# Tile 2's threshold by taking away eight smallest scores sixteen times, and a priority for each kind of step in attention's list

## The chip, the cores and the metric

The kernel runs on one core of a Trainium2 chip. A core has a matrix engine (TensorE, in the profile PE, with its weight loads as PEld), a vector engine (VectorE, DVE), an activation engine (ScalarE, ACT), a general engine (GpSimd, POOL) and a queue that issues transfers (SyncE, SP). They run side by side and wait for each other by semaphores. The metric is the device time of one execution, in microseconds.

## The reference

One decoder layer for 1024 tokens of width 1024. A conditioning vector gives shifts, scales and gates. One input projection gives q, k, v for 8 heads of 64, the queries, keys and weights of a small indexer, and 512 pooling channels. The indexer scores every earlier token for every query, and attention sees only the best 256:

```python
score = jnp.einsum('bqh,bqhs->bqs', w, jax.nn.relu(logits))
score = jnp.where(causal[None], score, -jnp.inf)
_, idx = lax.top_k(score, k_sel)          # k_sel = 256
...
s = jnp.where(valid[:, None], s, -jnp.inf)
p = jax.nn.softmax(s, axis=-1)
o = jnp.einsum('bhqk,bqkhd->bhqd', p, vg.astype(jnp.float32))
```

Attention and pooling go through an output projection, a gated residual and a layer norm; then a SwiGLU with inner width 2816, a second gated residual and a second layer norm.

## The kernel before, in words

The 1024 queries are 8 tiles of 128 (numbered 0 to 7). Tile i has 128 (i + 1) keys in causal reach. Tiles 0 and 1 have at most 256 and need no selection. For tiles 2 to 7 the kernel makes the indexer's scores (`score(i)`, fp32, one row for each query), finds the 256th largest score of each row as a threshold, and then overwrites the scores with a mask: 0 where the key is taken, a large negative number where not. Attention adds the mask to its own scores.

**The threshold** is found bit by bit in `bisect` (line 569). A first pass counts the scores that are not negative, which gives the sign. Then a search over 15 bits of the upper half of the fp32 word and one over 16 bits of the lower half: for each bit a pass over the row compares keys (16-bit integers in `keys[i]`) with a candidate and counts, and two small instructions set the next candidate. In `search_v` (line 600) all of this runs on DVE, in `search_a` (line 614) the pass and the small steps run on ACT. Tiles 3 and the pair 5, 4 are searched on ACT, tile 2 and the pair 7, 6 on DVE. The end of `bisect` (lines 648 to 666) makes the mask: equal and less-than flags, a scan that settles ties from the right, and the final product.

`bisect` is a generator: each `yield` names an engine and an estimate of the next piece. Before attention, `fill` (line 702) puts pieces into gaps of the projections. Tile 2's search is the late one (`LATE`, line 49): it takes pieces only when tiles 7 and 6 are done.

**Attention** has 32 units, from the largest tiles down: (7, 6) for four head pairs, then (5, 4), (3, 2), (1, 0). A unit, in `unit` (line 1199), has these steps, each a task of a list:

- `s`: scores of two heads on PE, into one or two of the two wide banks.
- `x`: scores plus mask, with the row maximum, on DVE (in the profile CUSTOM_DVE_ANT_0, sm from s and score). Frees the bank.
- `e`: exponential with row sum, on ACT.
- `r`: reciprocal on DVE. `n`: the product with it on POOL.
- `p`: transposes of the probabilities on PE, up to four to a bank (pT). `c`: the copy out of that bank, on ACT or DVE.

For each head pair follow `o` (the product with v on PE), `hi` (rounded copy on ACT) and `lo` (the remainder on DVE). `q_rows` (line 1162) prepares the queries of tiles 5 to 0: `load` from memory, `turn` (transposes on PE), and copies `own` and `other` on ACT and `low` on DVE, written to qab. Banks for `turn`, `p` and `o` come from a ring of four.

**The order** is written out by a planner that runs while the kernel is built (lines 1300 to 1378). It keeps a clock for each engine, knows what every task needs, and picks, again and again, the task that can start earliest; among equal starts the lowest rank goes first, where the rank of unit k's tasks is about 10 k. A piece of a search that is not finished is a candidate too (`Chain`, line 1284), with a rank that rises toward the unit that needs the mask. A task with two engines pays `V_BIAS` on the second: 0.15, on DVE. The order that comes out is fixed on PE, DVE, ACT and POOL; the engines keep it whatever the real durations are. An `x` task waits in the planner for its tile's mask, and `turn` for the masks whose buffers its output overwrites.

Behind the list come the output projection (`wo`), layer norm, and the SwiGLU, whose matmuls (`gu`, `dn`) fill TensorE to the end.

Every instruction goes through one helper, so the profile gives line 178 for nearly all; they are told apart by the names of their tiles.

Of the kernel before, what the change touches and what calls it, by code (L numbers as in the profile page):

```python
# [20 lines left out]
P = 128  # L21
# [19 lines left out]
EAGER = 0  # L41
Q_LEAD = 40
CHAIN_LEAD = 1
V_BIAS = 0.15
AHEAD_SMALL = 2
NORM = 2
NORM_SMALL = 2
# [87 lines left out]
class Queue:  # L135
# [6 lines left out]
    def cost(self, op, aps, k):  # L142
        out, n = aps[0], 1
        for s_ in out.shape[1:]:
            n *= s_
        if self.name == "T":
            if op == "transpose":
                return 0.13
            return max(n * (0.000443 if aps[1].dtype == F32R else 0.0000131 * aps[1].shape[-1]), 0.11)
        if self.name == "A":  # L150
            return max(0.26, 0.14 + n * 0.00088) + (0.31 if "accum_out" in k else 0)
        if self.name == "G":
            return 0.12 + n * {"tensor_tensor": 0.00225, "scalar_tensor_tensor": 0.0014}.get(op, 0.00125)
        if out.dtype in (BF16, I16, U16) and op in ("tensor_scalar", "tensor_tensor", "tensor_copy"):
# [36 lines left out]
def decoder_layer_kernel(  # L191
# [23 lines left out]
    def buf(where, off, n, name, dt=F32):  # L215
        return nc.alloc_sbuf_tensor_at(f"{name}_{where}{off}", [P, n], dt, offset=area[where] + 4 * off).ap()
# [327 lines left out]
    def score(i):  # L544
        return XS[:, s_off[i] : s_off[i] + P * (i + 1)]
# [21 lines left out]
    biased, hold = set(), []  # L567

    def bisect(tiles, cols, on_act):

        nt = len(tiles)
        col = lambda q: cols[:, q * 4 : q * 4 + nt]
# [4 lines left out]
        def trash(i):  # L577
            return ((junkA if 5 in tiles else junkB) if on_act else junkd(i))[:, 0 : P * (i + 1)]
# [67 lines left out]
        V.tensor_tensor(th.bitcast(I32), th.bitcast(I32), ib.bitcast(I32), ALU.bitwise_or)  # L646
        V.tensor_tensor(M, th, sg, ALU.mult)
        for m, i in enumerate(tiles):
            n = P * (i + 1)
            sc = score(i)  # L650
            T1 = one(M, m)
            eq, lt = kv[i].bitcast(BF16), trash(i)
            yield "V", 1.7 * w_(i) + 0.1

            V.tensor_scalar(eq, sc, T1, None, ALU.is_equal)
            V.tensor_scalar(lt, sc, T1, float(TOPK - n), ALU.is_lt, ALU.add, accum_out=one(ng, m))
            V.tensor_scalar(one(ng, m), one(ng, m), -0.5, None, ALU.add)
            yield "V", 1.6 * w_(i)
            left = sc.bitcast(BF16)[:, 0:n]
            V.tensor_tensor_scan(left[:, ::-1], eq[:, ::-1], eq[:, ::-1], one(ng, m), ALU.add, ALU.bypass)  # L660
            V.tensor_scalar(left, left, 0.0, None, ALU.is_lt)
            yield "V", 1.8 * w_(i)
            V.tensor_tensor(eq, eq, left, ALU.mult)
            V.tensor_tensor(lt, lt, eq, ALU.max)
            V.tensor_scalar(sc, lt, NOT_TAKEN, None, ALU.mult)
            biased.add(i)


    queues = {"V": V, "A": A, "G": G}
# [450 lines left out]

    class Task:

        def __init__(self, q, cost, rank, emit, deps=(), slots="", late=0.0):
            self.q, self.cost, self.rank, self.emit, self.deps, self.slots, self.late = q, cost, rank, emit, deps, slots, late
            self.end, self.kind, self.masks = None, emit.__name__[0:2], ()

    class Ring:

# [33 lines left out]
    def q_rows(t, rank):  # L1162
        hold_ = {}

        def load():
            hold_["raw"] = q_load(t)

        def turn():
            hold_["pt"] = q_transpose(hold_["raw"])

        b = qab[t]
        qa, ql = b[:, 0:1024], b[:, 1024:1536]
        qops[t] = qa, ql
# [15 lines left out]
        l_ = task("S", 0.1, rank, load, q_turns[-3:-2], late=4.0)  # L1189
        t_ = task("T", 0.55, rank, turn, (l_,), "A", late=0.2)  # L1190
        c0 = task("A", 1.2, rank, lambda: copies(0), (t_,))
        lw = task("V", 1.4, rank, lambda: copies(2), (c0,))
        c1 = task("A", 1.2, rank, lambda: copies(1), (c0,))
        t_.readers = (c1, lw)
        t_.masks = {1: (2, 3), 0: (4, 5)}.get(t, ())
        q_done[t] = (c1, lw)
        q_turns.append(t_)

    def unit(k):
# [23 lines left out]
        xs = [task("V", 0.08 + 0.00105 * n, 10 * k, lambda e=e: x_(e), [s_t] + before, late=0.12) for e in (0, 1)]  # L1223
        for x in xs:
            x.masks = (i,)
        s_t.readers = xs
        es = [task("A", 0.16 + 0.00097 * n, 10 * k + 1, lambda e=e: e_(e), (xs[e],), late=0.15) for e in (0, 1)]
        r_ = task("V", 0.15, 10 * k + 1, lambda: V.reciprocal(cols["c"][:, 2:4], cols["c"][:, 2:4]), es, late=0.15)
        ns = [task("G", 0.1 + 0.001 * n, 10 * k + 2, lambda e=e: n_(e), (r_,), late=0.15) for e in (0, 1)]
        ps, cs = [], []  # L1230
        for e in (0, 1):
            for j0 in range(0, i + 1, 4):
# [13 lines left out]
                    else:  # L1246
                        A.activation(dst, pv, AF.Copy)

                p = task("T", 0.107 * m, 10 * k + 3, p_, (ns[e],), "A", late=0.25)
                c = task("AV", (0.09 + 0.11 * m, 0.09 + 0.13 * m), 10 * k + 3, c_, [p] + list(o_tasks[-2:-1]), late=0.1)  # L1250
                p.readers = (c,)
                ps.append(p)
                cs.append(c)
# [8 lines left out]
    for k in range(0, nu, 2):  # L1262
# [15 lines left out]
        h_t = task("A", 0.3, 10 * k + 15, hi_, (o_t,), late=0.1)  # L1278
        l_t = task("V", 0.38, 10 * k + 16, lo_, (h_t,), late=0.1)
        o_t.readers = (l_t,)  # L1280
        o_tasks.append(o_t)
    goal = {2: 17, 3: 16, 4: 9, 5: 8, 6: 1, 7: 0}

    class Chain:

        def __init__(self, st):
            self.st, self.at, self.n = st, 0.0, -1
            nt = len(st[3])
            total = 6 * nt + 1 + (31 * (nt + 1) + 2 if st[5] else 31 * nt)
            self.left = max(total - st[6], 1)  # L1290
            self.goal = max(goal[i] for i in st[3]) - CHAIN_LEAD
# [13 lines left out]
    for i in biased:  # L1305
        masked[i] = 0.0
    chains = [Chain(st) for st in streams]
    todo.sort(key=lambda t: t.rank)
    kind = [""]

    def earliest(t, q):
# [29 lines left out]
            for r in t.readers:  # L1341
                held_by.setdefault(id(r), []).append(t)
    while todo or chains:
        best = None
        for t in todo:
            if best is not None and t.rank > best[3] + 400:
                break
            for n_q, q in enumerate(t.q):
                at = earliest(t, q)
                if at >= FAR:  # L1350
                    continue
                key = (at + (V_BIAS if n_q else 0.0), t.rank)
                if best is None or key < best[0]:
                    best = key, t, q, t.rank, at, n_q
        for c in chains:
            at = max(clock[c.q], c.at)
            key = (at, c.rank)
            if best is None or key < best[0]:
                best = key, c, c.q, c.rank, at, 0
        _, t, q, _, at, n_q = best  # L1360
        if t in chains:
            run_chain(t, at)
            continue
# [754 lines left out]
```

## Time and profile before

| what | value |
|---|---|
| median of three runs | 1258.84 us (1257.67 to 1259.99) |
| the profiled execution | 1260.96 us |
| its span, first to last instruction | 1259.2 us |
| PE busy | 1185.7 us, 94% |
| DVE busy | 999.6 us, 79% |
| ACT busy | 668.3 us, 53% |
| POOL busy | 708.3 us, 56% |
| granted TensorE clock, mean | 0.976 |

Busy times are of one profiled execution. Attention runs from about 334 us (the last projection's matmuls end there) to about 477 us. In a group of instructions the line reads: source line, engine, operation, output and inputs by the program's names, shapes, count, then total busy time and the mean of one in ns, then the idle time before them and what ended it. In a table of stretches each engine's busy time is followed by its count of instructions.

### The profile page before, as it was taken

The page shows a single profiled execution, that of the slowest core. Times are in us where ns is not written, and L with a number is a line of the kernel's source. Part 1 is how long each engine was busy: PE and PEld are TensorE (multiplying, and loading weights), DVE is VectorE, ACT ScalarE, POOL GpSimd, SP SyncE. Part 2 cuts the span into 40 slices and gives each one's busy share as a digit, 9 for nine tenths or more (in the row PEclk, how much of TensorE's full clock was granted, in tenths as well). Part 3 has the DMA queues.
Part 4 walks back from the last instruction along what each step waited for, and adds up shares of the span by engine and source line. Part 5 has one row for each costly group of instructions (what it writes and reads, how often), then busy time and mean ns, then how long its engine had stood idle before and what let it go on. Part 6 is the DMA issues. An engine that isn't in the chain of part 4 may idle for free.

```text
span 1259.2 us, 16396 instructions
## 1 busy us (share of the span) xinstructions
PE 1185.7 (94%) x5622; PEld 921.1 (73%) x5622; DVE 999.6 (79%) x1829; ACT 668.3 (53%) x1364; POOL 708.3 (56%) x505
## 2 busy tenths in 40 slices
PE   8999989999868999996899999999999999999996
PEld 6756556687645667886778787878878787878775
DVE  6798997988988865776877878787777768687697
ACT  4667878887788784355343333343333333332521
POOL 0193474675024453286773848384756657486848
PEclk9999999999978999997999999999999999999998
DMA  9610167411100035100202010101111120202112
GB/s 353 243 51 17 55 238 273 159 55 59 42 34 18 1 137 178 47 9 34 101 17 85 33 68 34 67 34 68 53 48 68 34 87 31 84 34 101 67 50 117
DMA packets 32459, 103.40 MB, mean 82 GB/s; under 512 B 3572, under 2 KB 3572, under 8 KB 28792
## 3 DMA queue, kind: packets, MB, share of 16 engines
q1 hardware_dynamic: 32376, 102.36, 22.3%
q8 instruction: 44, 0.72, 0.2%
q14 instruction: 39, 0.32, 0.1%
HBM read 92.90 MB, written 9.45 MB: 81 GB/s over the span
## 4 chain that ended last, share of the span: by engine, by line
PE 38%; DVE 7%; POOL 5%; issue 2%; ACT 1%; DVEq 0%; POOLq 0%; ACTq 0%
PE gu L178 23%; PE dn L178 15%; DVE act_W L178 2%; DVE utmp_X L178 2%; POOL wraw_R L178 1%; POOL wblk_T L178 1%; POOL wraw_W L178 1%; POOL wblk_V L178 1%; DVE gtmp_V L178 1%; DVE wblk_T L178 1%; DVE hr_H L178 0%; POOL hr_H L178 0%; DVE stat_C L178 0%; DVE wblk_V L178 0%; DVE res_X L178 0%
## 5 line engine op out<-in xcount | busy, mean ns | idle before, releaser
L178 PE MATMUL gu<-hr_H,wblk_V 128*128 128x512 f32 (+1 forms) x924 | 216.7, 386 | 2.4 <-ACT gtmp_V L178 1.8
L178 PE MATMUL gu<-hr_H,wblk_T 128*128 128x512 f32 (+1 forms) x924 | 216.1, 385 | 2.6 <-ACT gtmp_V L178 2.3
L178 PEld LDWEIGHTS gu<-hr_H,wblk_V 128*128 128x128 f32 x924 | 171.1, 189 | 39.1 <-ACT gtmp_V L178 2.2
L178 PEld LDWEIGHTS gu<-hr_H,wblk_T 128*128 128x128 f32 x924 | 170.7, 189 | 39.1 <-ACT gtmp_V L178 3.2
L178 DVE TENSOR_TENSOR res_X<-res_X,dn 128x512 f32<-128x512 f32 (+1 forms) x253 | 158.4, 674 | 15.4 <-PE dn L178 15.3
L178 POOL TENSOR_TENSOR wraw_R<-wraw_R 128x512 f32<-128x512 f32 x64 | 93.9, 1475 | 45.8 <-DVE wblk_T L178 23.1
L178 POOL TENSOR_TENSOR wraw_W<-wraw_W 128x512 f32<-128x512 f32 x60 | 86.2, 1444 | 58.3 <-DVE wblk_V L178 28.7
L178 PE MATMUL pj<-ws_W,hT_H 128*128 128x512 f32 x456 | 115.6, 400 | 1.0 <-DVE ws_W L178 1.0
L178 POOL TENSOR_SCALAR sm_H<-sm_H,stat_X 128x1024 f32<-128x1024 f32 (+7 forms) x64 | 48.5, 774 | 110.4 <-DVE stat_X L178 106.4
L178 PEld LDWEIGHTS pj<-ws_W,hT_H 128*128 128x128 f32 x456 | 83.0, 188 | 24.9 <-issue 6.6
L178 PE MATMUL dn<-wblk_T,act_W 128*128 128x512 f32 x324 | 79.4, 393 | 1.6 <-POOL wblk_T L178 1.1
L178 PE MATMUL dn<-wblk_V,act_W 128*128 128x512 f32 x324 | 79.1, 393 | 1.1 <-POOL wblk_V L178 1.1
L178 DVE TENSOR_SCALAR_CACHE_REDUCE junk_X<-keysD_T,colsD_X 128x1024 int16<-128x1024 int16 (+1 forms) x64 | 79.4, 1268 | 0.2
L178 ACT ACTIVATE wblk_V<-wraw_R 128x512 fp32r<-128x512 f32 x56 | 35.3, 630 | 79.7 <-POOL wraw_R L178 67.0
L178 ACT ACTIVATE wblk_V<-wraw_W 128x512 fp32r<-128x512 f32 x53 | 33.1, 627 | 75.0 <-POOL wraw_W L178 61.5
L178 PEld LDWEIGHTS dn<-wblk_T,act_W 128*128 128x128 f32 x324 | 60.2, 188 | 17.2 <-POOL wblk_T L178 3.9
L178 PEld LDWEIGHTS dn<-wblk_V,act_W 128*128 128x128 f32 x324 | 60.1, 188 | 16.6 <-POOL wblk_V L178 3.9
L178 ACT ACTIVATE wblk_T<-wraw_W 128x512 fp32r<-128x512 f32 x56 | 35.0, 628 | 67.2 <-POOL wraw_W L178 56.2
L178 ACT ACTIVATE wblk_T<-wraw_R 128x512 fp32r<-128x512 f32 x52 | 32.5, 628 | 60.4 <-POOL wraw_R L178 47.7
L178 ACT ACTIVATE utmp_X<-gu 128x512 f32<-128x512 f32 x33 | 19.7, 598 | 74.0 <-PE gu L178 74.0
L178 DVE SCALAR_TENSOR_TENSOR score_X<-relu_K,const_C,score_X 128x384 f32<-128x384 f32 (+5 forms) x42 | 54.1, 1289 | 5.0 <-ACT relu_K L178 1.4
L178 PE MATMUL pT<-const_C,sm_H 128*128 128x128 f32 x288 | 45.9, 305 | 12.8 <-POOL sm_H L178 4.1
(303 smaller groups left out, 2734.9 us busy)
## 6 DMA issues: line engine op xcount, KB each, us to landing
mset_K<-in_wmr_dram SPq DMA_DIRECT2D x16, 1024.0 KB, 5.2
wm_K<-in_wma_dram SPq DMA_DIRECT2D x16, 512.0 KB, 10.0
wraw_R<-in_wg_dram SPq DMA_DIRECT2D x6, 1024.0 KB, 4.7
wraw_R<-in_wd_dram SPq DMA_DIRECT2D x12, 512.0 KB, 3.5
wraw_W<-in_wup_dram SPq DMA_DIRECT2D x12, 512.0 KB, 3.5
wraw_R<-in_wup_dram SPq DMA_DIRECT2D x10, 512.0 KB, 3.6
wraw_W<-in_wg_dram SPq DMA_DIRECT2D x5, 1024.0 KB, 4.8
wraw_W<-in_wd_dram SPq DMA_DIRECT2D x10, 512.0 KB, 3.5
```

Of the source, the lines that this page charges most:

```text
L178: ins_ = f(*a, **k)
```

## The change

Two parts, and numbers.

**Tile 2's threshold.** Tile 2 has 384 keys in reach of 256 wanted, so the 256th largest is what is left as the smallest once 128 are taken away. The new `drop_eights` negates the scores into a buffer of its own, and sixteen times finds the eight largest of the negated row and replaces them by a very small number. A last maximum gives the threshold. The mask's steps are moved, unchanged, into `mask_steps`, which `bisect` uses as well. Tile 2's 16-bit keys and scratch buffer go, and its small columns move (`colsE` to where the keys were).

**The list.** Every kind of task gets an offset to its rank (`PRIO`), and each search that is still running gets a first rank and a step (`CHAIN_PRIO`) in place of a goal. The planner gathers all tasks that can start within 0.106 us (`SPAN`) of the earliest and takes the one of lowest rank. `V_BIAS` becomes -0.075. The cost estimates of `s` and `o` and of a search piece on ACT change. `turn` of tile 1 no longer waits for tile 2's mask.

```diff
-V_BIAS = 0.15
+V_BIAS = -0.075
+SPAN = 0.106
+PRIO = {'load': -387, 'turn': -49, 'own': -168, 'low': -13, 'other': -88, 's': 3, 'x': -36, 'e': 1, 'r': 152, 'n': -121, 'p': 12, 'c': 332, 'o': -134, 'hi': -115, 'lo': 145}
+CHAIN_PRIO = {2: (500, 22.3), 3: (347, 6.4), 4: (-732, 10.2)}
...
-    junks[2] = buf("X", 7296, 192, "junk").bitcast(BF16)
-    colsE = buf("X", 7232, 64, "colsE")
-    keys = {2: kA[:, 0:192], 3: kA[:, 192:448], 4: k4, 5: k5, 6: kD[:, 0:448], 7: kD[:, 448:960]}
+    colsE = buf("X", 4224, 64, "colsE")
+    keys = {3: kA[:, 192:448], 4: k4, 5: k5, 6: kD[:, 0:448], 7: kD[:, 448:960]}
...
+    def drop_eights(i, cols):
+
+        n = P * (i + 1)
+        neg = buf("X", 4800, n, "neg")
+        m8, ng, T1 = cols[:, 0:8], cols[:, 8:9], cols[:, 9:10]
+        yield "V", 0.5
+        V.tensor_scalar(neg, score(i), -1.0, None, ALU.mult)
+        for r in range((n - TOPK) // 8):
+            yield "V", 1.0
+            V.max(m8, neg)
+            V.match_replace(neg, m8, neg, -3.4e38)
+        yield "V", 0.7
+        V.max(m8, neg)
+        V.tensor_scalar(T1, m8[:, 0:1], -1.0, None, ALU.mult)
+        halves = neg.bitcast(BF16)
+        yield from mask_steps(i, T1, ng, halves[:, 0:n], halves[:, n : 2 * n])
...
     def bisect(tiles, cols, on_act):
 
+        if tiles == LATE:
+            yield from drop_eights(tiles[0], cols)
+            return
...
-        t_.masks = {1: (2, 3), 0: (4, 5)}.get(t, ())
+        t_.masks = {1: (3,), 0: (4, 5)}.get(t, ())
...
-        s_t = task("T", 0.1 + 0.0014 * n, 10 * k - EAGER, s_, q_done[i], "B" if n <= 512 else "BB", late=0.2)
+        s_t = task("s", "T", 0.2 + 0.0014 * n, 10 * k - EAGER, s_, q_done[i], "B" if n <= 512 else "BB", late=0.2)
...
-        o_t = task("T", 0.1 + 0.43 * (g + 1), 10 * k + 14, o_, cs, "A", late=0.3)
+        o_t = task("o", "T", 0.1 + 0.865 * (g + 1), 10 * k + 14, o_, cs, "A", late=0.3)
...
-            self.rank = 10 * self.goal * (self.n + 1) / self.left
+            first, step = CHAIN_PRIO[self.st[3][-1]]
+            self.rank = first + step * self.n
             self.q = self.st[1][0]
-            self.cost = 1.08 * self.st[1][1]
+            self.cost = (0.95 if self.q == "A" else 1.08) * self.st[1][1]
...
     while todo or chains:
-        best = None
+        can = []
         for t in todo:
...
             for n_q, q in enumerate(t.q):
                 at = earliest(t, q)
...
+                if at < FAR:
+                    can.append((at + V_BIAS * n_q, t.rank, len(can), t, q, at, n_q))
         for c in chains:
             at = max(clock[c.q], c.at)
...
+            can.append((at, c.rank, len(can), c, c.q, at, 0))
+        soon = min(can)[0] + SPAN
+        _, _, _, t, q, at, n_q = min((c for c in can if c[0] <= soon), key=lambda c: (c[1], c[0], c[2]))
```

More of the change, by code (lines that the diff above doesn't have):

```diff
@@ L153, in cost @@
             return 0.12 + n * {"tensor_tensor": 0.00225, "scalar_tensor_tensor": 0.0014}.get(op, 0.00125)
+        if op == "max":
+            return 0.08 + aps[1].shape[-1] * 0.00106
         if out.dtype in (BF16, I16, U16) and op in ("tensor_scalar", "tensor_tensor", "tensor_copy"):
@@ L560, in decoder_layer_kernel, with mask_steps @@
     junkB = buf("X", 6976, 256, "junkB").bitcast(BF16)
-    junks[2] = buf("X", 7296, 192, "junk").bitcast(BF16)
     colsD = buf("X", 8576, 64, "colsD")
-    colsE = buf("X", 7232, 64, "colsE")
-    keys = {2: kA[:, 0:192], 3: kA[:, 192:448], 4: k4, 5: k5, 6: kD[:, 0:448], 7: kD[:, 448:960]}
+    colsE = buf("X", 4224, 64, "colsE")
+    keys = {3: kA[:, 192:448], 4: k4, 5: k5, 6: kD[:, 0:448], 7: kD[:, 448:960]}
     keys = {i: kw.bitcast(I16) for i, kw in keys.items()}
     biased, hold = set(), []
+    def mask_steps(i, T1, ng, eq, lt):
+        n, sc, w = P * (i + 1), score(i), (i + 1) / 8
+        yield "V", 1.7 * w + 0.1
+        V.tensor_scalar(eq, sc, T1, None, ALU.is_equal)
+        V.tensor_scalar(lt, sc, T1, float(TOPK - n), ALU.is_lt, ALU.add, accum_out=ng)
+        V.tensor_scalar(ng, ng, -0.5, None, ALU.add)
+        yield "V", 1.6 * w
+        left = sc.bitcast(BF16)[:, 0:n]
+        V.tensor_tensor_scan(left[:, ::-1], eq[:, ::-1], eq[:, ::-1], ng, ALU.add, ALU.bypass)
+        V.tensor_scalar(left, left, 0.0, None, ALU.is_lt)
+        yield "V", 1.8 * w
+        V.tensor_tensor(eq, eq, left, ALU.mult)
+        V.tensor_tensor(lt, lt, eq, ALU.max)
+        V.tensor_scalar(sc, lt, NOT_TAKEN, None, ALU.mult)
+        biased.add(i)
+    def drop_eights(i, cols):
[13 more added lines that the diff above has]
+        yield from mask_steps(i, T1, ng, halves[:, 0:n], halves[:, n : 2 * n])
     def bisect(tiles, cols, on_act):
+        if tiles == LATE:
+            yield from drop_eights(tiles[0], cols)
+            return
         nt = len(tiles)
@@ L648, in bisect @@
         for m, i in enumerate(tiles):
[L649 to L666, printed above, removed]
+            yield from mask_steps(i, one(M, m), one(ng, m), kv[i].bitcast(BF16), trash(i))
     queues = {"V": V, "A": A, "G": G}
@@ L1121, in decoder_layer_kernel, with __init__ @@
     class Task:
-        def __init__(self, q, cost, rank, emit, deps=(), slots="", late=0.0):
-            self.q, self.cost, self.rank, self.emit, self.deps, self.slots, self.late = q, cost, rank, emit, deps, slots, late
-            self.end, self.kind, self.masks = None, emit.__name__[0:2], ()
+        def __init__(self, kind, q, cost, rank, emit, deps=(), slots="", late=0.0):
+            self.q, self.cost, self.rank, self.emit, self.deps, self.slots, self.late = q, cost, rank + PRIO[kind], emit, deps, slots, late
+            self.end, self.kind, self.masks = None, kind, ()
     class Ring:
@@ L1187, in copies @@
                 V.tensor_tensor(lv[64:128], pv[64:128], f_(qv[64:128, :, 1, :]), ALU.subtract)
[L1189 to L1193, printed above, removed]
+        l_ = task("load", "S", 0.1, rank, load, q_turns[-3:-2], late=4.0)
+        t_ = task("turn", "T", 0.55, rank, turn, (l_,), "A", late=0.2)
+        c0 = task("own", "A", 1.2, rank, lambda: copies(0), (t_,))
+        lw = task("low", "V", 1.4, rank, lambda: copies(2), (c0,))
+        c1 = task("other", "A", 1.2, rank, lambda: copies(1), (c0,))
         t_.readers = (c1, lw)
-        t_.masks = {1: (2, 3), 0: (4, 5)}.get(t, ())
+        t_.masks = {1: (3,), 0: (4, 5)}.get(t, ())
         q_done[t] = (c1, lw)
@@ L1219, in n_ @@
             G.tensor_scalar(sms[e], sms[e], cols["c"][:, 2 + e : 3 + e], 0.0, ALU.mult, ALU.add)
-        s_t = task("T", 0.1 + 0.0014 * n, 10 * k - EAGER, s_, q_done[i], "B" if n <= 512 else "BB", late=0.2)
+        s_t = task("s", "T", 0.2 + 0.0014 * n, 10 * k - EAGER, s_, q_done[i], "B" if n <= 512 else "BB", late=0.2)
         before = [t for w in where for t in sm_users.get(w, ())]
-        xs = [task("V", 0.08 + 0.00105 * n, 10 * k, lambda e=e: x_(e), [s_t] + before, late=0.12) for e in (0, 1)]
+        xs = [task("x", "V", 0.08 + 0.00105 * n, 10 * k, lambda e=e: x_(e), [s_t] + before, late=0.12) for e in (0, 1)]
         for x in xs:
@@ L1226, in unit @@
         s_t.readers = xs
-        es = [task("A", 0.16 + 0.00097 * n, 10 * k + 1, lambda e=e: e_(e), (xs[e],), late=0.15) for e in (0, 1)]
-        r_ = task("V", 0.15, 10 * k + 1, lambda: V.reciprocal(cols["c"][:, 2:4], cols["c"][:, 2:4]), es, late=0.15)
-        ns = [task("G", 0.1 + 0.001 * n, 10 * k + 2, lambda e=e: n_(e), (r_,), late=0.15) for e in (0, 1)]
+        es = [task("e", "A", 0.16 + 0.00097 * n, 10 * k + 1, lambda e=e: e_(e), (xs[e],), late=0.15) for e in (0, 1)]
+        r_ = task("r", "V", 0.15, 10 * k + 1, lambda: V.reciprocal(cols["c"][:, 2:4], cols["c"][:, 2:4]), es, late=0.15)
+        ns = [task("n", "G", 0.1 + 0.001 * n, 10 * k + 2, lambda e=e: n_(e), (r_,), late=0.15) for e in (0, 1)]
         ps, cs = [], []
@@ L1247, in c_ @@
                         A.activation(dst, pv, AF.Copy)
-                p = task("T", 0.107 * m, 10 * k + 3, p_, (ns[e],), "A", late=0.25)
-                c = task("AV", (0.09 + 0.11 * m, 0.09 + 0.13 * m), 10 * k + 3, c_, [p] + list(o_tasks[-2:-1]), late=0.1)
+                p = task("p", "T", 0.107 * m, 10 * k + 3, p_, (ns[e],), "A", late=0.25)
+                c = task("c", "AV", (0.09 + 0.11 * m, 0.09 + 0.13 * m), 10 * k + 3, c_, [p] + list(o_tasks[-2:-1]), late=0.1)
                 p.readers = (c,)
@@ L1275, in lo_ @@
             V.tensor_tensor(ca[:, 1024 + pr * 256 : 1024 + (pr + 1) * 256], hold_["po"][:, 0:256], f_(ca[:, pr * 256 : (pr + 1) * 256]), ALU.subtract)
-        o_t = task("T", 0.1 + 0.43 * (g + 1), 10 * k + 14, o_, cs, "A", late=0.3)
-        h_t = task("A", 0.3, 10 * k + 15, hi_, (o_t,), late=0.1)
-        l_t = task("V", 0.38, 10 * k + 16, lo_, (h_t,), late=0.1)
+        o_t = task("o", "T", 0.1 + 0.865 * (g + 1), 10 * k + 14, o_, cs, "A", late=0.3)
+        h_t = task("hi", "A", 0.3, 10 * k + 15, hi_, (o_t,), late=0.1)
+        l_t = task("lo", "V", 0.38, 10 * k + 16, lo_, (h_t,), late=0.1)
         o_t.readers = (l_t,)
         o_tasks.append(o_t)
-    goal = {2: 17, 3: 16, 4: 9, 5: 8, 6: 1, 7: 0}
     class Chain:
@@ L1287, in __init__ @@
             self.st, self.at, self.n = st, 0.0, -1
[L1288 to L1291, printed above, removed]
             self.step()
@@ L1307, in decoder_layer_kernel @@
     chains = [Chain(st) for st in streams]
-    todo.sort(key=lambda t: t.rank)
     kind = [""]
@@ L1343, in decoder_layer_kernel @@
     while todo or chains:
-        best = None
+        can = []
         for t in todo:
-            if best is not None and t.rank > best[3] + 400:
-                break
             for n_q, q in enumerate(t.q):
                 at = earliest(t, q)
[L1350 to L1354, printed above, removed]
+                if at < FAR:
+                    can.append((at + V_BIAS * n_q, t.rank, len(can), t, q, at, n_q))
         for c in chains:
             at = max(clock[c.q], c.at)
[L1357 to L1360, printed above, removed]
+            can.append((at, c.rank, len(can), c, c.q, at, 0))
+        soon = min(can)[0] + SPAN
+        _, _, _, t, q, at, n_q = min((c for c in can if c[0] <= soon), key=lambda c: (c[1], c[0], c[2]))
         if t in chains:
```

## The prediction

> **What bounds the kernel now.** I read the page's head and its 40 slices first, then a table of stretches around attention, then what TensorE waited for in them, then the groups of instructions of tile 2's search.
>
> ```profile
> span 1259.2 us, 16396 instructions
> PE   8999989999868999996899999999999999999996
> PEclk9999999999978999997999999999999999999998
> ```
>
> TensorE sets the pace in most slices. The dip in slices 11 and 12 (31.5 us each) is the start of attention, the stage that the change touches. The next rows are stretches: length, then the busy time of PE, PEld, DVE, ACT and POOL, then the granted clock and DMA.
>
> ```profile
> 334.00:395.00 61.00, 42.93 (x230) 28.07 (x228) 51.68 (x152) 53.32 (x114) 17.32 (x14) 0.80 0.09 31
> 395.00:436.00 41.00, 39.27 (x309) 27.61 (x306) 36.17 (x107) 35.19 (x88) 18.20 (x17) 1.00 0.04 14
> 436.00:477.00 41.00, 39.53 (x289) 26.57 (x287) 26.58 (x104) 35.34 (x111) 24.67 (x38) 1.00 0.36 129
> 477.00:563.00 86.00, 85.72 (x402) 70.57 (x402) 57.24 (x125) 37.99 (x72) 39.55 (x27) 1.00 0.21 74
> ```
>
> In the first 61 us TensorE is idle for 18.1 us and its clock is 0.80, while DVE is busy for 51.7 us and ACT for 53.3 us. From 395 us on TensorE is busy for 96% (39.27 of 41), and in the output projection from 477 us for 99.7%. So only the first stretch has time to give, and what comes off attention moves the rest forward whole: the projection follows without a gap. What TensorE waited for there (total, times, longest):
>
> ```profile
> PE s L178 <- DVE stat_X L178: 4.7, 6, 2.1
> PE pT L178 <- ACT qab_W L178: 3.4, 1, 3.4
> PE pT L178 <- POOL sm_H L178: 3.3, 2, 2.8
> PE pT L178 <- ACT pT_H L178: 3.2, 3, 1.2
> ```
>
> It waits for DVE to empty score banks and for ACT to get round to copies: both are shared with the threshold searches. The two searches that still run are tile 2's (DVE: keysA with colsE) and tile 3's (ACT: keysA with colsA):
>
> ```profile
> L178 DVE TENSOR_SCALAR_CACHE_REDUCE junk_X<-keysA_X,colsE_X 128x384 int16<-128x384 int16 (+1 forms) x32 | 21.4, 668 | 0.6
> L178 DVE TENSOR_SCALAR colsE_X<-colsE_X 128x1 f32<-128x1 f32 (+1 forms) x64 | 11.7, 183 | 2.2
> L178 ACT ACTIVATE junkB_X<-keysA_X,colsA_X 128x512 bf16<-128x512 uint16 x14 | 10.1, 719 | 0.2
> L178 ACT ACTIVATE colsA_X<-colsA_X 128x1 f32<-128x1 f32 x28 | 8.2, 294 | 0.5
> L178 ACT ACTIVATION_READ_ACCUMULATOR junkB_X<-keysA_X,colsA_X 128x1 f32 x14 | 2.7, 193 | 0.0
> ```
>
> Tile 3's search holds ACT for 10.1 + 8.2 + 2.7 = 21.0 us, 1.5 us for each of 14 bits. Its mask has a due time, too:
>
> ```profile
> 431.38 0.49 DVE L178 TENSOR_SCALAR keysA_X<-score_X,colsA_X 128x512 bf16<-128x512 f32 x1
> 436.69 0.43 DVE L178 TENSOR_SCALAR score_X<-junkB_X 128x512 f32<-128x512 bf16 x1
> 437.67 0.69 DVE L178 CUSTOM_DVE_ANT_0 sm_H<-s,score_X 128x512 f32<-128x512 f32 x1 [0.42 <-PE s L178]
> ```
>
> The mask is finished at 437.1 us (431.38 to 436.69 + 0.43: 5.7 us for its own steps), and the first masked maximum of tile 3 starts at 437.67. So up to 436 us the stage is a race of ACT (53.32 + 35.19 = 88.5 us busy of 102), DVE (87.9) and TensorE (82.2).
>
> **Tile 2's threshold: what goes.** One bit of the old search is a pass, a read of its count and two small instructions:
>
> ```profile
> 351.50 0.65 DVE L178 TENSOR_SCALAR_CACHE_REDUCE junk_X<-keysA_X,colsE_X 128x384 int16<-128x384 int16 x1
> 352.08 0.08 DVE L178 DVE_READ_ACCUMULATOR junk_X<-keysA_X,colsE_X 128x1 f32 x1
> 352.20 0.40 DVE L178 TENSOR_SCALAR colsE_X<-colsE_X 128x1 f32<-128x1 f32 x2
> 352.64 0.67 DVE L178 TENSOR_SCALAR_CACHE_REDUCE junk_X<-keysA_X,colsE_X 128x384 int16<-128x384 int16 x1
> ```
>
> From 351.50 to 352.64 is 1.14 us a bit. The 32 passes (31 bits and one count between the halves) make 36.5 us; with the one instruction that builds the low keys (0.62, below) 37.1 us leave DVE. The mask's own steps stay.
>
> **What comes.** One negation, 16 rounds of a maximum and a replacement, a last maximum and a small instruction. No row has a maximum of eight or a replacement, so I bound both by what DVE does with 384 elements here:
>
> ```profile
> L178 DVE TENSOR_SCALAR keysA_X<-score_X,colsE_X 128x384 bf16<-128x384 f32 x1 | 0.4, 421 | 0.0
> L178 DVE CUSTOM_DVE_ANT_0 sm_H<-s,score_X 128x384 f32<-128x384 f32 x8 | 4.2, 552 | 3.3 <-POOL sm_H L178 3.3
> L178 DVE SCALAR_TENSOR_TENSOR keysA_X<-keysA_X,colsE_X,score_X 128x384 uint16<-128x384 int16 x1 | 0.6, 619 | 0.0
> L178 DVE TENSOR_TENSOR_SCAN score_X<-keysA_X,colsE_X 128x384 bf16<-128x384 bf16 x1 | 1.0, 999 | 0.0
> ```
>
> From below 0.42 us each, a round 0.84; from above the scan's 1.00 each plus one small instruction of 0.18 to take in the eight values, a round 2.18. I take 0.55, because that row is fp32 in and out, runs over each element once and ends in a maximum, with 0.15 for the eight values: 1.25 us a round. Sum: 0.42 + 16 x 1.25 + 0.55 + 0.18 = 21.2 us; ends 14.5 and 36.5. DVE is relieved of 37.1 - 21.2 = **15.9 us**, ends 22.6 and 0.6.
>
> The Trainium skill ("VectorE: DVE Perf Modes", Two Vector instructions with no wait between them) speaks against the change here: it counts a replacement as two instructions, a load of the values and the replacement. No run here shows it yet; by that count a round has three instructions, and if the load cost as much as a small one the sum would be 0.5 us larger.
>
> **The list: who takes what is freed.** Freed DVE time helps TensorE's first wait directly; for ACT it must be handed over. The copies of transposed probabilities may go to either, and the change's bias turns from 0.15 against DVE to 0.075 for it. The copies as they are:
>
> ```profile
> L178 ACT ACTIVATE pT_H<-pT 128x512 f32<-128x512 f32 x45 | 25.8, 599 | 3.7 <-PE pT L178 3.3
> L178 DVE COPY pT_H<-pT 128x512 f32<-128x512 f32 x3 | 2.0, 682 | 0.0
> ```
>
> A copy costs about as much on either, so the sum of both engines up to 436 us goes from 88.5 + 87.9 = 176.4 to 160.5 us, 80.25 each if the copies level it, some 14 of them moved. ACT's busy share was 88.5 / 102 = 0.868; at the same share 80.25 us take 92.5, **9.5 us less**. With the ends of DVE's relief (0.6, 22.6) it is 0.7 and 13.4 us. TensorE must fit under 92.5 us, and does: its 82.2 us hold a slow clock, as the transposes show (80 at the low clock, 208 after):
>
> ```profile
> 334.00:395.00 61.00, 16.74 (x80) 12.61 (x80) 0.00 (x0) 11.22 (x21) 0.80 0.09 31
> 395.00:477.00 82.00, 28.93 (x208) 22.14 (x208) 5.19 (x11) 25.60 (x62) 1.00 0.20 72
> ```
>
> At 28.93 / 208 = 0.139 us each, 80 would take 11.1 us, 5.6 less. That is the second term. Filling TensorE's gaps should lift the clock in part; nothing here bounds how far but 0 and 5.6, and I take the middle, 2.8, less 0.5 for DVE's slower copies (14 x 0.08 is 1.1, shared by two engines): **2.3 us**.
>
> The Trainium skill ("TensorE: Matmul & The Clock Gate", The HAM clock gate) lets the clock fall after an idle window of about 3.4 us. The trace agrees so far as it goes, its longest wait there being 3.4 us; by that rule all waits below the window would return the whole 5.6 us, and the sum would be 2.8 us better.
>
> The priorities themselves reorder everything within 0.106 us of the earliest start. They add no instruction. Tile 2's rounds go last (500 and up), tile 3's bits next to last (347 and up), tile 5 and 4's remaining mask first (-732), copies late (332). I cost the order at nothing; its cover is the slack of DVE and ACT, 14 us each of the 102, and what it costs without that is the last rival. The queue loads come earlier (-387); each is one issue on a queue that is mostly empty. Tile 1's q rows no longer wait for tile 2's mask, which is worth nothing while both masks come before them. After 436 us TensorE is full, so I expect nothing there.
>
> **Sum.** 9.5 + 2.3 = 11.8 us off the profiled execution's 1260.96 (span 1259.2 and 1.8 around it): 1249.2. The three runs' median is 1258.84, 2.1 lower, so the forecast is 1258.84 - 11.8 = **1247**.
>
> **Rivals.** *TensorE becomes the bound at once.* Then the 102 us shrink to TensorE's work at full clock and 96% busy: (82.2 - 5.6) / 0.96 = 80 us, 22 less, 1237. For it: after 395 us it runs so. Against: ACT and DVE would both need 80.25 us of 80.
>
> *The relief does not arrive*, because a round costs the upper end, or because ACT keeps its copies and tile 3's 21.0 us. Then 0 to 5 us, about 1256. For it: ACT is as loaded as DVE, and the old chain's DVE time is not ACT's.
>
> *Slower: the masks come late.* Both remaining searches now stand behind nearly everything, and tile 3's is serial. When tile 4's last unit is through and bits are left, they run alone at 1.5 us each plus 5.7 us of mask steps, with TensorE empty. From 5 bits left (13.2 us) the gain is gone; with 10 left it is 20.7 - 11.8 = 8.9 us lost, 1268. For it: before, the mask was ready only 0.6 us ahead of use, and the units in front now come sooner. Against: ACT's copies get out of its way.
>
> **Chances.** Forecast 0.62 (1240, with both terms at their better ends, 13.4 + 5.6, to 1253, half the sum), TensorE-bound 0.09, no arrival 0.15, late masks 0.14. About 0.2%, 2.5 us, is what a measurement of this kernel tells from no change. Of the 0.15 half is within that: faster 0.78, same 0.08, slower 0.14. The range goes down to 1236 and up to 1260, which leaves out most of the slower case.
>
> **What would show it.** Right: DVE shows 17 maxima and 16 replacements of about 0.55 us, with no colsE passes; more copies on DVE than 11; first stretch at a clock above 0.80; the projection starting near 465 instead of 477; the stretches behind it unchanged in length. Wrong: rounds near 2 us; TensorE idle for over 5 us just before tile 3's first masked maximum; ACT still at 88 us with TensorE waiting for its copies.

## The result and the profile after

The changed kernel's median is 1251.93 us (1250.99 to 1254.49) beside 1258.84 us (1257.12 to 1259.99), five runs each: a ratio of 0.994, 95% interval 0.9926 to 0.9953. That is faster by 6.9 us where 11.8 were forecast, and inside the range. The profiled execution took 1250.99 us, 9.97 below the one of before; of those, 2.1 us are by how much before's profiled execution lay above its own median, and 0.9 by how much this one lies below its.

The head of the page, with the slices of TensorE and of its granted clock:

```profile
span 1249.2 us, 16310 instructions
PE   8999989999888899997899999999999999999996
PEclk9999999999989899997999999999999999999998
```

Slices 11 to 14 of TensorE were 8, 6, 8 and 9 and are 8, 8, 8 and 8; the clock's were 9, 7, 8 and 9 and are 9, 8, 9 and 8. So the dip is filled in part, and slice 14 (406 to 437 us), which was full, has lost some. The same four stretches as before, with the same columns (length, busy time and count of PE, PEld, DVE, ACT and POOL, clock, DMA):

```profile
334.00:395.00 61.00, 52.27 (x354) 36.31 (x354) 53.19 (x119) 54.96 (x118) 21.34 (x20) 0.92 0.07 23
395.00:436.00 41.00, 32.66 (x210) 22.10 (x206) 39.16 (x95) 29.16 (x70) 18.08 (x15) 0.88 0.11 39
436.00:477.00 41.00, 40.56 (x294) 28.58 (x293) 29.08 (x105) 31.24 (x97) 21.45 (x35) 1.00 0.35 123
477.00:563.00 86.00, 82.76 (x388) 68.19 (x386) 58.38 (x137) 40.60 (x81) 40.83 (x28) 1.00 0.21 71
```

The counts of matmuls tell more than the busy times. By 395 us the changed kernel has issued 354 where before had issued 230: a lead of 124. In the next 41 us it issues 210 where before issued 309, and the lead shrinks to 25 (in the projection a matmul takes about 0.21 us, 85.72 us for 402, so 25 are worth some 5 us). The stretch that was full is now the one with a hole: 8.3 us idle at a clock of 0.88.

From the start of attention to the last head pair's product (`o`, at 477.66 before and 471.43 after), the one row is before and the other after:

```profile
334.00:477.70 143.70, 122.42 (x825) 82.58 (x823) 114.78 (x363) 124.54 (x312) 60.19 (x69) 0.92 0.15 54
```

```profile
334.00:471.40 137.40, 119.89 (x823) 82.50 (x821) 117.53 (x311) 112.12 (x278) 60.86 (x69) 0.93 0.16 57
```

For the same work (the two counts differ by two of 825) attention is 6.3 us shorter: TensorE is busy for 2.5 us less (122.42 - 119.89) and idle for 3.8 us less (21.28 - 17.51). The other 3.7 us between the two profiled executions arise behind attention, where nothing was changed. From the first matmul of the SwiGLU (`gu`) to the end, the fourteen profiled executions of this study take between 677.7 and 683.8 us for the same work, and not in the order of their attention: 682.6 before, 677.9 after, 678.2 with the list alone, the slowest kernel. So I count the 3.7 us as scatter of single executions; it fits the 3.0 us by which the two lie off their medians.

Tile 2's search as groups (shortest, median and longest duration in ns, first and last start), and one of its rounds with the start of the next in the timeline of DVE (start, duration). The helper that issues nearly everything is line 183 in this kernel, and 180 or 183 in those of the experiments:

```profile
L183 DVE MAX8 colsE_X<-neg_X x17: 540/554/562, 337.8 to 420.6; 128x8 f32<-128x384 f32 x17
L183 DVE MATCH_VALUE_LOAD neg_X<-colsE_X,neg_X x16: 84/92/93, 338.4 to 405.3; 128x8 f32 x16
L183 DVE MATCH_REPLACE8 neg_X<-colsE_X,neg_X x16: 541/542/546, 338.4 to 405.4; 128x384 f32<-128x384 f32 x16
```

```profile
337.76 0.56 DVE L183 MAX8 colsE_X<-neg_X 128x8 f32<-128x384 f32 x1
338.36 0.09 DVE L183 MATCH_VALUE_LOAD neg_X<-colsE_X,neg_X 128x8 f32 x1
338.44 0.54 DVE L183 MATCH_REPLACE8 neg_X<-colsE_X,neg_X 128x384 f32<-128x384 f32 x1
339.01 0.56 DVE L183 MAX8 colsE_X<-neg_X 128x8 f32<-128x384 f32 x1
```

A round takes 339.01 - 337.76 = 1.25 us, the estimate to the digit. What TensorE waited for from 318 to 480 us (total, times, longest), the first rows of before and then those of after:

```profile
PE s L178 <- DVE stat_X L178: 6.2, 10, 2.1
PE pT L178 <- POOL sm_H L178: 4.1, 3, 2.8
```

```profile
PE pT L183 <- POOL sm_H L183: 8.2, 5, 3.3
PE pT L183 <- DVE pT_H L183: 2.7, 4, 1.1
PE pT L183 <- ACT pT_H L183: 2.7, 3, 1.1
PE s L183 <- DVE stat_X L183: 1.7, 3, 0.9
```

DVE's score banks are no longer what it waits for most; POOL's normalized probabilities are.

### The profile page after: what moved, and what is told of

Read it like the earlier page. It is cut to its first block, busy times and chain, and to the rows that moved or that the text cites. A ratio compares the mean times of both kernels' runs of the same rounds, so it can differ in the third digit from the quotient of the medians.

```text
span 1249.2 us, 16310 instructions
## 1 busy us (share of the span) xinstructions
PE 1180.4 (94%) x5622; PEld 919.8 (74%) x5622; DVE 1002.0 (80%) x1772; ACT 656.0 (53%) x1330; POOL 709.3 (57%) x505
## 4 chain that ended last, share of the span: by engine, by line
PE 38%; DVE 7%; POOL 5%; issue 2%; ACT 1%; DVEq 0%; POOLq 0%; ACTq 0%
PE gu L183 23%; PE dn L183 15%; DVE act_W L183 2%; DVE utmp_X L183 2%; POOL wraw_R L183 1%; POOL wblk_T L183 1%; POOL wraw_W L183 1%; POOL wblk_V L183 1%; DVE gtmp_V L183 1%; DVE wblk_T L183 1%; DVE hr_H L183 0%; POOL hr_H L183 0%; DVE stat_C L183 0%; DVE wblk_V L183 0%; DVE res_X L183 0%
```

## The experiments

The twelve kernels take parts of the change alone, or alter the kernel after in one place or two. The expectations name the theories by letters. A: both parts of the change are needed. B: the list alone brings the gain. C: the threshold alone does. D: W_o's multiplications on POOL cost the lead. E: the list's own order costs it. F: the copies hand DVE's relief over. G: the priorities put it to use. H and I are the two sides of whether a truer estimate of a round helps the planner. J: late masks cost the lead. K: orders of equal cost scatter. L: the priorities as such are the gain.

One table carries most of the readings: the lead in matmuls over before, counted from the same rows of stretches (before had issued 230 by 395 us, 539 by 436 and 828 by 477), and the time.

| kernel | by 395 | by 436 | by 477 | median less before's, us | ratio, 95% interval |
|---|---|---|---|---|---|
| after | +124 | +25 | +30 | -6.9 | 0.9940 (0.9926 to 0.9953) |
| threshold alone | -7 | -4 | -28 | +2.4 | 1.0014 (1.0001 to 1.0026) |
| threshold and copies | +2 | -64 | -54 | +8.0 | 1.0068 (1.0056 to 1.0080) |
| list alone | +139 | +68 | -100 | +12.6 | 1.0101 (1.0087 to 1.0115) |
| after, bias of before | +99 | +43 | +4 | -3.2 | 0.9979 (0.9970 to 0.9989) |
| after, searches first | -100 | -95 | -83 | +8.7 | 1.0075 (1.0063 to 1.0088) |
| after, no multiplications | +120 | +57 | +54 | -13.3 | 0.9901 (0.9886 to 0.9916) |
| after, multiplications later | +122 | +57 | +50 | -11.5 | 0.9911 (0.9899 to 0.9924) |
| the same, truer round | +118 | +5 | +10 | -2.1 | 0.9985 (0.9976 to 0.9994) |
| span 0.09 | +72 | -7 | +2 | -1.2 | 0.9986 (0.9975 to 0.9998) |
| span 0.09, later | +80 | -3 | -12 | -0.9 | 0.9997 (0.9986 to 1.0008) |
| span 0.12 | +117 | +17 | +16 | -4.8 | 0.9966 (0.9954 to 0.9978) |
| span 0.12, later | +124 | +33 | +26 | -8.0 | 0.9932 (0.9915 to 0.9949) |

Every kernel with the priorities and the short search placed late is 70 to 125 matmuls ahead at 395 us, and no other but the list alone is. The time follows what is left of the lead at 477 us, nearly in order.

**The threshold alone.** The kernel before with the new search, `mask_steps`, their buffers, a planner's cost for the new maximum (the change has it too), and `turn` of tile 1 without the wait for tile 2's mask. Under the old list the search needs its count of pieces for its goal:

```diff
             total = 6 * nt + 1 + (31 * (nt + 1) + 2 if st[5] else 31 * nt)
+            if st[3] == LATE:
+                total = 21
             self.left = max(total - st[6], 1)
```

> The kernel before with the new threshold for tile 2 alone; list, biases and costs as before. Theory A (DVE relief and copies handed over are both needed): DVE is relieved of some 16 us, but ACT keeps its copies, so about half of the sum's first term arrives: 4 to 6 us less than before, 1253 to 1255. Theory B (the list alone did it): within 2 us of before, 1257 to 1260. Theory C (the threshold alone did it): as the changed kernel, 1251 to 1253.

1261.24 us, 1.0014: no gain, though DVE was relieved. It lies just above B's range and outside those of A and C. Its rows of the first two stretches, and tile 2's last mask step:

```profile
334.00:395.00 61.00, 41.71 (x223) 27.10 (x222) 50.45 (x108) 51.56 (x112) 18.27 (x14) 0.75 0.09 31
395.00:436.00 41.00, 39.79 (x312) 28.43 (x312) 28.37 (x71) 34.60 (x82) 18.60 (x18) 1.00 0.08 27
384.06 1.06 DVE L180 TENSOR_SCALAR score_X<-neg_X 128x384 f32<-128x384 bf16 x1
```

In the first stretch DVE is as busy as before (50.45 beside 51.68): the old list used the relief to finish the mask at 385 us, some 36 us sooner than before's 420.7. The relief came out in the second stretch (28.37 beside 36.17), where TensorE had been full already. The forecast's first term needs it in the first.

**The list alone.** The kernel after with the old search for tile 2. It has more pieces, so its step in rank is smaller:

```diff
-CHAIN_PRIO = {2: (500, 22.3), 3: (347, 6.4), 4: (-732, 10.2)}
+CHAIN_PRIO = {2: (500, 12.3), 3: (347, 6.4), 4: (-732, 10.2)}
...
-        if tiles == LATE:
-            yield from drop_eights(tiles[0], cols)
-            return
```

> The changed kernel with tile 2's threshold found bit by bit again (its rank step 12.3 for 38 pieces in place of 22.3 for 21). Theory A: copies move to a DVE that still carries the old search, so DVE becomes the bound: 0 to 5 us slower than before, 1258 to 1264. Theory B: 1251 to 1254. Theory C: within 2 us of before.

1271.44 us, 1.0101, the slowest of all, with the largest lead at 395 us. A had the sign, at less than half the size (at most 5 us slower); B and C fall. Where it went stands in one row of TensorE's timeline:

```profile
457.80 1.95 PE L183 MATMUL s<-kr_K,qab_H 128*128 128x512 f32 x4 [19.26 <-DVE stat_X L183]
```

TensorE stood still for 19.26 us until tile 2's mask was there (its last step ends at 456.66 us) and DVE had emptied a score bank with it. This is the prediction's slower rival in pure form, for the other search. So the priorities make the early lead, the 36 us of the old search don't fit behind it, and the 21 us of the new one nearly do: theory A, by a way that the prediction didn't have.

**The copies.** Two kernels turn `V_BIAS` alone. The first is the threshold alone with the new bias:

```diff
-V_BIAS = 0.15
+V_BIAS = -0.075
```

> The kernel before with the new threshold and with the changed bias for copies (-0.075), the rest of the list as before. Theory F (the sum's first term: the freed DVE time reaches ACT through the copies): 6 to 10 us less than before, 1249 to 1253. Theory G (the priorities are what uses it: they push the searches back and let the first head pairs run): within 3 us of before, 1256 to 1261.

The second is the kernel after with the old one:

```diff
-V_BIAS = -0.075
+V_BIAS = 0.15
```

> The changed kernel with the bias for copies at 0.15 as before; priorities and threshold stay. Theory F: the gain goes, 1256 to 1261. Theory G: most of it stays, 1250 to 1255.

With the threshold alone the new bias moves copies as it should (55 on DVE, 41 on ACT) and makes the kernel slower, 1267.20 us, 1.0068. Neither theory had that, and why it is slower stays open. Under the priorities the old bias keeps 99 of the 124 matmuls of lead by 395 us with 33 copies on DVE, and ends at 1256.08 us, 0.9979. That lies at the edge of F's range and outside G's: less than half of the time gained is left (3.2 of 6.9 us). So handing copies over doesn't turn relief into time by itself (F falls with the first kernel), and the priorities make the lead without it (G holds for the lead, not for the time). With them the bias is worth 3.7 us by the medians, less than neighbouring orders differ by (below).

**The searches first.** Is the gain in pushing the searches back, or did their lateness cost some of it?

```diff
-CHAIN_PRIO = {2: (500, 22.3), 3: (347, 6.4), 4: (-732, 10.2)}
+CHAIN_PRIO = {2: (-400, 10.0), 3: (-600, 6.4), 4: (-732, 10.2)}
```

> The changed kernel with the two remaining searches ahead of nearly everything (first ranks -600 for tile 3 and -400 for tile 2 in place of 347 and 500). Theory G: the first head pairs wait again as in the kernel before, the third head pair's product comes near 398 us instead of 381, and the gain is gone: 1256 to 1262. Theory J (late masks cost more than an early start brings): 1247 to 1251, tile 3's and tile 2's masks done by 400 us.

1267.93 us, 1.0075. The masks are done by 368.2 us, and until then TensorE all but stands, busy for 5.2 us of the 38 from 334 to 372: its longest wait for DVE is 30.8 us.

```profile
PE s L183 <- DVE stat_X L183: 35.6, 8, 30.8
```

From 372 to 500 us it is then busy for 121.3 of 128 us, and its 16 products run from 391.2 to 488.1, 97 us, where after takes 111 (360.1 to 471.4) and before 112. Pushing the searches back makes the early lead, and J as a whole falls. G has the direction but was too mild: the third head pair's product starts at 409.7 us, not near 398, and the time lies 6 us above its range. With the searches out of the way the products' stretch is 14 us shorter than after's: that is an upper estimate of what the lateness of the masks still costs, as in those 97 us DVE and ACT carry no search at all.

**W_o's first blocks.** Where did the 124 go between 395 and 436 us? The rows suspected are those that prepare the output projection's weights: a gate multiplication on POOL, a rounded copy on ACT, a remainder on DVE. They aren't tasks of the list; they come behind it in the program, run when their buffer and their engine come free, and the planner's clocks don't know them.

Two kernels. The first leaves the multiplications of blocks 0 to 3 out, so that these blocks of the projection are not gated:

```diff
-        G.tensor_tensor(wo_raw[k], wo_raw[k], GR, ALU.mult)
+        if k > 3:
+            G.tensor_tensor(wo_raw[k], wo_raw[k], GR, ALU.mult)
```

> The changed kernel without the gate's multiplication of the first four blocks of the output projection's weight on POOL (left out, so the projection is not gated there). Theory D (the lead of 17.5 us that the changed kernel has at the third head pair is lost because POOL's multiplications, which the planner does not count, stretch the mask's steps on DVE, 2.44 us for one that takes 0.42, and hold up normalizations): the mask's steps fall to 0.36 to 0.5 us, the stall of 3.3 us at 419 us goes, 4 to 8 us come back, 1244 to 1248. Theory E (the lead is lost by the list's own order around the masks): within 2 us of the changed kernel, 1250 to 1253.

The second does all the work, with the loads and multiplications of blocks 0 to 2 as tasks of the list that wait for the masks of tiles 2 and 3:

```diff
+    loaded = [t for t in todo if t.kind == "load"]
+    for k in range(3):
+        w_t = task("w", "G", 2.4, 300 + k, lambda k=k: wo_load(k), loaded + [q_turns[3 + k]], late=0.1)
+        w_t.masks = (2, 3)
...
-    wo_load(0)
...
-    wo_load(1)
-    wo_load(2)
```

> The changed kernel with the multiplications of the first three blocks made tasks of the list, held until the masks of tiles 2 and 3 are done, so that no work is left out. Theory D: most of what leaving them out gives, 3 to 6 us under the changed kernel, 1246 to 1249, with tile 3's mask done some 4 us sooner after its last bit. Theory E: 1250 to 1253.

0.9901 and 0.9911 (1245.51 and 1247.30 us, both as D had it): both faster than after, and the second is the best kernel of the study with all its work done, 1247.3 us. Its products and those of after start alike up to the fourth (392.81 and 392.74 us). Then, of after, the timelines of POOL, ACT and DVE:

```profile
389.30 2.38 POOL L183 TENSOR_TENSOR raw_R<-raw_R,gr_G 128x1024 f32<-128x1024 f32 x1 [1.13 <-DMA raw_R<-in_wo_dram]
391.71 1.06 ACT L183 ACTIVATE wo_V<-raw_R 128x1024 fp32r<-128x1024 f32 x1 [1.65 <-POOL raw_R L183]
396.78 1.21 DVE L183 TENSOR_TENSOR wo_V<-raw_R,wo_V 128x1024 fp32r<-128x1024 f32 x1
...
417.14 2.37 POOL L183 TENSOR_TENSOR raw_R<-raw_R,gr_G 128x1024 f32<-128x1024 f32 x1 [2.92 <-PE pT L183]
417.35 2.44 DVE L183 TENSOR_TENSOR keysA_X<-keysA_X,score_X 128x512 bf16<-128x512 bf16 x1
...
429.14 2.39 POOL L183 TENSOR_TENSOR raw_R<-raw_R,gr_G 128x1024 f32<-128x1024 f32 x1 [5.91 <-issue]
430.21 1.54 DVE L183 TENSOR_TENSOR neg_X<-neg_X,score_X 128x384 bf16<-128x384 bf16 x1
433.75 0.69 DVE L183 CUSTOM_DVE_ANT_0 sm_H<-s,score_X 128x512 f32<-128x512 f32 x1
```

and the same steps of the kernel with the multiplications later:

```profile
413.46 0.42 DVE L183 TENSOR_TENSOR keysA_X<-keysA_X,score_X 128x512 bf16<-128x512 bf16 x1
...
424.35 0.34 DVE L183 TENSOR_TENSOR neg_X<-neg_X,score_X 128x384 bf16<-128x384 bf16 x1
...
426.73 0.69 DVE L183 CUSTOM_DVE_ANT_0 sm_H<-s,score_X 128x512 f32<-128x512 f32 x1
```

Tile 3's first masked maximum comes 433.75 - 426.73 = 7.0 us later in after. The pieces can be read off (the faster kernel does block 0's steps at 426 to 439 us, as the last mask step ends). ACT waits 1.65 us for block 0's multiplication and copies for 1.06, with the exponentials queued behind; DVE waits for those and then makes the remainder, 1.21: DVE is 2.5 us behind at its next search round. Two mask steps in SBUF beside a multiplication take 2.44 and 1.54 us for 0.42 and 0.34: 3.2 us. The other 1.3 come in smaller pieces. While DVE is inside such a step, what queues behind it is the reciprocal for the next unit, so POOL's product is late, and TensorE waits for that:

```profile
422.40 2.21 PE L183 MATMUL pT<-const_C,sm_H 128*128 128x128 f32 x10 [3.34 <-POOL sm_H L183]
```

So this wait names POOL, and the late one is DVE. What the collisions cost TensorE shows in the row from the start of attention to the last product of the kernel with the multiplications later:

```profile
334.00:466.60 132.60, 117.08 (x822) 80.23 (x820) 115.75 (x313) 110.59 (x275) 61.44 (x69) 0.95 0.17 59
```

It is 4.8 us shorter than the row of after (137.40). TensorE is idle for 2.0 us less (15.52 beside 17.51) and busy for 2.8 us less (117.08 beside 119.89, at a clock of 0.95 beside 0.93), so the larger half is matmuls that run faster, not waits. D is right for this order. E has the rest: without the multiplications, too, the lead falls from 120 to 57 by 436 us.

**A truer round.** The kernel above, with the planner told what a round costs (1.16 x 1.08 = 1.25 us):

```diff
-            yield "V", 1.0
+            yield "V", 1.16
```

> The kernel with the gate's multiplications held until the masks are done, and the planner's cost of a round raised from 1.08 to 1.25 us, as measured. Theory H (the planner's remaining slip comes from the round's cost: 16 x 0.17 = 2.7 us): 1 to 3 us under that kernel, 1244 to 1246. Theory I (the slip has other sources): within 1.5 us of it, 1246 to 1249.

1257.14 us, 0.9985: the order made with the better number is worse by 9 us, outside both H and I. Its lead at 395 us is much the same (+118), at 436 us it is 5. TensorE's largest wait and one mask step say why in part:

```profile
PE s L183 <- DVE stat_X L183: 14.0, 11, 5.8
427.43 2.38 DVE L183 TENSOR_SCALAR score_X<-neg_X 128x384 f32<-128x384 bf16 x1
```

Two multiplications, issued at 424.74 for 4.86 us, fell on tile 2's last mask steps after all: two of them took 2.38 us each in place of 0.36, 4.0 us more. The rest of the 9 us is not taken apart here. That left the question how much of any one number here belongs to the idea, and how much to the one order that a parameter hits.

**Other orders of the same work.** `SPAN` a little smaller and a little larger, each with the multiplications as they are and later:

```diff
-SPAN = 0.106
+SPAN = 0.09
```

```diff
-SPAN = 0.106
+SPAN = 0.12
```

> The changed kernel with SPAN 0.09 in place of 0.106, which makes another order of the same work. It measures how far the time scatters with the order alone. Theory K (a good part of the gain belongs to this one order): 5 us or more from the changed kernel, 1257 or above. Theory L (the gain belongs to the priorities): 1249 to 1255.

> The same with the gate's multiplications held until the masks are done. Theory D (the multiplications cost the lead): 3 to 6 us less than with SPAN 0.09 alone. Theory K: a difference of either sign.

> The changed kernel with SPAN 0.12. Theory K: 5 us or more from the changed kernel. Theory L: 1249 to 1255.

> The same with the gate's multiplications held until the masks are done. Theory D: 3 to 6 us less than with SPAN 0.12 alone. Theory K: a difference of either sign.

With the multiplications as they are the three orders (0.09, 0.106 and 0.12) take 0.9986, 0.9940 and 0.9966: the idea is worth 1.2 to 6.9 us by which order it falls into. By the ranges set beforehand 0.09 (1258.39 us) speaks for K and 0.12 (1254.81 us) for L. Holding them back brings 4.6 us by the medians at 0.106, 3.2 at 0.12 and nothing at 0.09. The collision explains the last, too. At 0.09 tile 2's last mask steps run undisturbed to begin with, and holding the multiplications back puts two of them right there; the first rows are span 0.09, the second ones the same with the multiplications later:

```profile
421.80 0.36 DVE L183 TENSOR_TENSOR neg_X<-neg_X 128x384 bf16<-128x384 bf16 x1
422.19 0.36 DVE L183 TENSOR_SCALAR score_X<-neg_X 128x384 f32<-128x384 bf16 x1
```

```profile
420.03 4.93 POOL L183 TENSOR_TENSOR raw_R<-raw_R,gr_G 128x1024 f32<-128x1024 f32 x2
420.31 2.41 DVE L183 TENSOR_TENSOR neg_X<-neg_X 128x384 bf16<-128x384 bf16 x1
422.76 2.43 DVE L183 TENSOR_SCALAR score_X<-neg_X 128x384 f32<-128x384 bf16 x1
```

4.84 us for 0.72. The planner let a multiplication start when it believed that the masks were done; the real order was behind its clock. So D holds as a mechanism, and its price belongs to one order. L holds for the early lead, which all orders have (+72 to +124), and not for how much of it is kept.

Neighbouring orders were run only for the whole change. There the three differ by 5.7 us, and by 10.6 with the multiplications later. The threshold, the copies and the list by themselves stand on one order each, so the 2.4 and 8.0 us of the first two say little of what another order would make of them. The searches first and the list alone rest on single waits of 30.8 and 19.3 us in their traces, which are larger than that.

## Why the prediction was right or wrong

**The round and the relief: right.** 17 maxima of 0.554 us, 16 replacements of 0.542, 1.25 us a round. The Trainium skill's count of two instructions for a replacement ("VectorE: DVE Perf Modes", Two Vector instructions with no wait between them) is what the trace shows: 16 MATCH_VALUE_LOAD of 0.092 us stand ahead of the 16 replacements, so three instructions a round, of which the load fits inside the 0.15 us that the estimate had for it. The instructions on tile 2's small columns, where the search keeps its state, hold DVE for 35.4 us before and 19.5 after, up to the mask's own steps (overlaps counted once); with the negation, which is not on them, 19.8. That is 15.6 us less where 15.9 were forecast. It did not arrive whole even as busy time: by the rows of attention above, DVE and ACT together are busy for 9.7 us less (239.3 to 229.7). As an estimate, the 34 more copies on DVE (11 before, 45 after) at 0.08 us more each take back 2.7 us, and the mask steps that stretched in after (below) some 4 more than those of before.

**The first term, 9.5 us: wrong in its mechanism.** The step that fails is "at the same share 80.25 us take 92.5": that the load of ACT and DVE sets the pace, and that levelling it by copies turns relief into time. Up to 436 us the load of both fell from 176.4 to 165.0 us in the kernel with the threshold alone, and was nearly levelled in the one with the copies (DVE 82.4, ACT 76.5); neither was faster. Nor did the two level in the kernel after: up to 436 us DVE went up to 92.4 us (53.19 + 39.16), and ACT down to 84.1. What set the pace of the start was which work stood ahead of which, as the searches first show. The measured counterpart of the term, TensorE's idle time, fell by 3.8 us.

**The clock, 2.3 us: right in size by luck, not in place.** TensorE's busy time fell by 2.5 us. But the first stretch got more than half of its clock back (0.80 to 0.92), and the second lost some (1.00 to 0.88). So the 2.5 us are a gain less a loss that the term didn't have, and "after 395 us it runs so" did not survive the change.

**"I cost the order at nothing": wrong both ways.** This is the step that decided. The order made the lead (+124 matmuls, of which the threshold alone makes none), and the order lost most of it. The named cover, 14 us of slack each on DVE and ACT, says nothing of when the slack is there. And the sum of attention's work left out W_o's preparation, which the list doesn't hold either: its first four multiplications went from 376, 381, 404 and 452 us to 389, 402, 417 and 429, the last two onto the masks. With the first three held back, a list that is alike up to there is 4.6 us faster.

**"After 436 us TensorE is full, so I expect nothing there": wrong.** Attention's end is where the gain is collected. The last product of tiles 5 and 4's group starts at 443.9 us in after, a little later than the 442.9 of before, and the last of all 6.2 us sooner: units behind the late mask had been worked ahead.

**The rivals.** TensorE did not become the bound (83% busy from 334 to 436 us by the two rows, beside 96% in that rival). "The relief does not arrive" is what the threshold alone did. "The masks come late" happened in part: tile 3's scores were ready at 430.6 and their maximum came at 433.75, behind tile 2's last mask step. The maximum was about 3 us late, where the rival had a serial 20.7 us, because the search was short; with the old search TensorE stood for 19.3 us in one wait. Of the prediction's own signs, the projection near 465 us did not come: the last product starts at 471.4. The sign came out right and the time, 4.9 us above the forecast, within the range, but with the lead's gain and its loss both missing from the sum, that is luck: with `SPAN` at 0.09 the same change brings 1.2 us.

## What to carry to other kernels

A shorter step on an engine that is shared brings time only if the order puts the freed time in front of what the bound engine waits for: ask at which microsecond the relief comes out, not only how large it is. Where an order is written out by a planner, list the work that the planner does not know and see what stands beside it on the chip; and before a gain of a few us is credited to an idea, run the same idea in two or three neighbouring orders. A lead counted in matmuls, stretch by stretch, shows gain and loss that a total hides.

## What was not expected of the hardware

A DVE instruction that starts while POOL is inside an elementwise instruction can stand until POOL is through, and the profile books this as DVE's busy time, not as a wait. The multiplication from 417.14 ends at 419.51; the DVE product that began at 417.35 ends at 419.79, 0.28 later. In the pair at 420.03, which ends at 424.96, the second DVE step ends at 425.19, 0.23 later. Beside POOL's shorter `sm` steps the same DVE steps take 0.94 and 0.95. The maxima of eight, the replacements and the steps that read score banks kept their times: in the kernels of the experiments and in after, those that began inside a multiplication took at most 0.561 us (7 maxima) and 0.543 (5 replacements), and the 21 masked maxima of 128x640 among them 0.82 in the median, as without one. The Trainium skill ("SBUF — State Buffer", Who interferes with whom) has the rule: DVE's second pair of ports is shared with GpSimd, whoever issues first holds it for the whole instruction, and the other is blocked, for a DVE instruction with two SBUF inputs or in a 2-port mode. The trace agrees, by the rows above; which mode an instruction ran in no run here shows. The prediction had not weighed it.

The clock fell without a long wait. The rows are stretches of after, all instructions:

```profile
399.00:403.00 4.00, 1.87 (x12) 1.27 (x13) 3.93 (x13) 2.98 (x9) 2.97 (x3) 0.90 0.37 131
403.00:410.00 7.00, 7.00 (x36) 4.55 (x36) 6.31 (x21) 5.90 (x15) 2.74 (x3) 0.57 0.01 2
```

TensorE was busy for 1.87 of 4 us, in waits of which none in its timeline is longer than 1.09 us, and in the next 7 us its clock was 0.57. The 24 matmuls of a product took 3.98 us there, and 2.60 in the kernel with the multiplications later. These are the same stretches of that kernel:

```profile
399.00:403.00 4.00, 3.22 (x29) 2.33 (x28) 3.97 (x13) 3.92 (x10) 0.84 (x2) 1.00 0.02 4
403.00:410.00 7.00, 5.11 (x45) 3.59 (x39) 6.79 (x21) 6.23 (x17) 2.81 (x4) 1.00 0.07 12
```

The prediction's second estimate of the clock term would have had all of it back as long as no wait was long. Here short waits, close together, went before a slow clock.
